# Rotating 96 images by 180 degrees: load packets of 64 KB and store packets of 32 KB, three on-chip columns and a scratch, instead of 32 KB and 16 KB with rotating tiles

## Chip, cores and metric

One core of one Trainium2 chip. The metric is the device time of one execution, in microseconds (us), as the median of several runs. Shorter is better. Terms: the DMA engines move data between HBM (the large memory) and the on-chip memory; in the traces they do so in packets, here of one row each; the span is the stretch of time that the profile covers.

## The reference

```python
def setup_inputs():
    batch, c, h, w = 32, 3, 256, 256
    return {"x": np.random.randn(batch, c, h, w).astype(np.float32)}

def reference(x):
    return np.rot90(x, k=2, axes=(-2, -1)).astype(np.float32)
```

Rotating an image by 180 degrees is the same as reversing the order of its 65,536 elements. There are 96 images of 256 KB: 25.17 MB are read from HBM and 25.17 MB written.

## The kernel before

Each of three passes takes 32 images. Every image is cut into 8 rows of 32 KB. Four of them are in tile `tinF`, the other four in reversed order in tile `tinB`, so that 32 x 4 rows fill the 128 partitions. VectorE copies half a row at a time with a negative step. Each half goes out as a store of its own (16 KB a row). Loads are issued on one queue (SyncE), stores on another (ScalarE).

```python
    NG = 32; Q = P // NG; S = 2 * Q; BLK = L // S; HB = BLK // 2
    x3 = x.rearrange("b c h w -> (b c) (h w)").rearrange("n (s e) -> n s e", s=S)
    o4 = out.rearrange("b c h w -> (b c) (h w)").rearrange(
        "n (s j f) -> n s j f", s=S, f=HB)
    tin_pool = ctx.enter_context(tc.tile_pool(name="tin", bufs=2))
    tout_pool = ctx.enter_context(tc.tile_pool(name="tout", bufs=4))
    for pp in range(n_pass):
        nsl = slice(pp * NG, (pp + 1) * NG)
        tinF = tin_pool.tile([P, BLK], x.dtype, tag="F")
        tinB = tin_pool.tile([P, BLK], x.dtype, tag="B")
        nc.sync.dma_start(out=tinF[:, :], in_=x3[nsl, 0:Q, :])
        nc.sync.dma_start(out=tinB[:, :], in_=x3[nsl, S - 1:Q - 1:-1, :])

        tF0 = tout_pool.tile([P, HB], x.dtype, tag="t")
        nc.vector.tensor_copy(out=tF0[:, :], in_=tinB[:, 2 * HB - 1:HB - 1:-1])
        nc.scalar.dma_start(out=o4[nsl, 0:Q, 0, :], in_=tF0[:, :])
        # [cut: the same for tB0 from tinF, tF1 from tinB, tB1 from tinF]
```

## Time and profile before

| | before |
|---|---|
| time, median (range), three runs | 123.76 us (123.72 to 123.96) |
| span in the profile | 122.3 us |
| VectorE busy | 27.2 us, 22% of the span |
| DMA queue 1 (loads) | 864 packets, 48.9% of the 16 DMA engines' span |
| DMA queue 10 (stores) | 1728 packets, 48.0% |
| HBM traffic | 50.33 MB, mean 412 GB/s |

The lines below are from the page of the kernel before: VectorE (DVE) busy time; the mean busy share of the DMA engines in 40 equal slices, in tenths; then for each DMA queue its packets, megabytes and share of the 16 engines' time.

```profile
DVE 27.2 (22%) x12; POOL 0.2 (0%) x4
...
DMA  5798989899999998999999999999999999999992
...
q1 hardware_dynamic: 864, 25.17, 48.9%
q10 hardware_dynamic: 1728, 25.17, 48.0%
```

The two shares add up to 97%: apart from the start and the end, the DMA engines are never free. Everything else must be read with that in mind. VectorE's waits are an example (the view of waits; total, number and longest, in us):

```profile
DVE tF L52 <- DMA tinB<-in_x_dram: 41.2, 2, 23.4
DVE tF L60 <- DMA out_dram<-tF: 14.7, 2, 12.2
DVE tB L56 <- DMA out_dram<-tB: 11.1, 2, 8.4
DVE tB L64 <- DMA out_dram<-tB: 7.6, 2, 5.0
DVE tF L52 <- DMA out_dram<-tF: 2.6, 1, 2.6
```

VectorE waits some 36 us for stores to free a tile. These waits look like something to remove, but while VectorE waits, the DMA engines are busy with what is already queued.

The trace keeps a start and a duration for every DMA packet. "Per engine" is a sum over all packets divided by 16.

### The profile page before, as it was taken

Reading aid. Unit: us, or ns where it says so; the run is one execution under the profiler, and the core shown is the slowest. Engines: PE = TensorE matmul, PEld = TensorE weight load, DVE = VectorE, ACT = ScalarE, POOL = GpSimd, SP = SyncE. Lnnn points to the kernel's source line nnn. Section 1 sums busy time; section 2 is a strip of 40 time slices with the busy share of each in tenths; the row PEclk is TensorE's granted clock in tenths of the full one; section 3 lists DMA queues with packets and bytes.
Section 4 is the critical chain, followed back from the end, with each engine's and each line's share of the span. In section 5 each row is a group of like instructions: output and inputs, shape, how many; then the busy total and the mean of one; then the engine's idle time right before and its main releaser. Section 6 shows DMA issues by size and latency. Waiting matters only on the chain.

```text
span 122.3 us, 93 instructions
## 1 busy us (share of the span) xinstructions
DVE 27.2 (22%) x12; POOL 0.2 (0%) x4
## 2 busy tenths in 40 slices
DVE  0000000399500000610160003307337156100000
POOL 0000000000000000000000000000000000000000
DMA  5798989899999998999999999999999999999992
GB/s 171 343 472 386 472 386 482 375 482 359 348 450 407 466 429 386 472 423 397 439 455 413 477 434 391 413 429 434 429 434 434 439 429 434 429 439 434 429 429 113
DMA packets 2592, 50.33 MB, mean 412 GB/s; under 512 B 288, under 2 KB 288, under 8 KB 288
## 3 DMA queue, kind: packets, MB, share of 16 engines
q1 hardware_dynamic: 864, 25.17, 48.9%
q10 hardware_dynamic: 1728, 25.17, 48.0%
HBM read 25.17 MB, written 25.17 MB: 412 GB/s over the span
## 4 chain that ended last, share of the span: by engine, by line
DMA 69%; DVE 11%; another core or an unknown queue 4%; SPq 0%; issue 0%; DVEq 0%
DMA out_dram<-tF 37%; DMA tinB<-in_x_dram 18%; DMA out_dram<-tB 14%; DVE tB L64 4%; DVE tF L60 4%; DVE tF L52 2%; DVE tB L56 2%; SPq L48 0%; DVEq L64 0%; DVEq L60 0%
## 5 line engine op out<-in xcount | busy, mean ns | idle before, releaser
L52 DVE COPY tF<-tinB 128x4096 f32<-128x4096 f32 x3 | 6.9, 2294 | 43.8 <-DMA tinB<-in_x_dram 41.2
L60 DVE COPY tF<-tinB 128x4096 f32<-128x4096 f32 x3 | 6.9, 2291 | 14.7 <-DMA out_dram<-tF 14.7
L56 DVE COPY tB<-tinF 128x4096 f32<-128x4096 f32 x3 | 6.9, 2292 | 11.1 <-DMA out_dram<-tB 11.1
L64 DVE COPY tB<-tinF 128x4096 f32<-128x4096 f32 x3 | 6.9, 2291 | 7.6 <-DMA out_dram<-tB 7.6
L80 POOL MEMSET const-bfloat16-1.0<- 128x1 bf16 x1 | 0.1, 102 | 0.0
L80 POOL MEMSET const-uint8-127<- 128x1 uint8 x1 | 0.1, 102 | 0.0
L80 POOL MEMSET const-float32-0.0<- 128x1 f32 x1 | 0.1, 99 | 0.2 <-issue 0.2
L80 POOL MEMSET const-float32-1.0<- 128x1 f32 x1 | 0.1, 99 | 0.0
## 6 DMA issues: line engine op xcount, KB each, us to landing
tinF<-in_x_dram SPq DMA_DIRECT2D x3, 4096.0 KB, 32.2
tinB<-in_x_dram SPq DMA_DIRECT2D x3, 4096.0 KB, 32.9
out_dram<-tF ACTq DMA_DIRECT2D x6, 2048.0 KB, 20.0
out_dram<-tB ACTq DMA_DIRECT2D x6, 2048.0 KB, 23.1
```

The costliest lines, as they stand in the source:

```text
L52: nc.vector.tensor_copy(out=tF0[:, :], in_=tinB[:, 2 * HB - 1:HB - 1:-1])
L56: nc.vector.tensor_copy(out=tB0[:, :], in_=tinF[:, 2 * HB - 1:HB - 1:-1])
L60: nc.vector.tensor_copy(out=tF1[:, :], in_=tinB[:, HB - 1::-1])
L64: nc.vector.tensor_copy(out=tB1[:, :], in_=tinF[:, HB - 1::-1])
L80: nc = _bacc.Bacc("TRN2", target_bir_lowering=False, num_devices=1)
```

## The change

The intent is larger packets and fewer waits. Each image is cut into 4 rows of 64 KB, so a group of 32 images fills a whole column of 128 x 64 KB. A row is loaded as one packet and stored as two of 32 KB. Three columns (A, B, C) and a scratch T hold everything: groups 0 and 2 are turned from A into C, group 1 inside B through T. The third load needs only the copies out of A, not a store.

```diff
-    x3 = x.rearrange("b c h w -> (b c) (h w)").rearrange(
-        "n (s e) -> n s e", s=S)
-    tin_pool = ctx.enter_context(tc.tile_pool(name="tin", bufs=2))
-    tout_pool = ctx.enter_context(tc.tile_pool(name="tout", bufs=4))
+    G = 32; E = L // 4; K = E // 4; J = E // 8      # [four lines joined]
+    x4 = x.rearrange("b c h w -> (b c) (h w)").rearrange(
+        "(g n) (s e) -> g (n s) e", n=G, s=4)
+    o4 = out.rearrange("b c h w -> (b c) (h w)").rearrange(
+        "(g n) (s e) -> g n s e", n=G, s=4)
+    # [cut: A, Bt, Ct are [P, E] tiles, T is [P, J], all from one pool with bufs=1]
+    # [cut: back(t, lo, hi) reads columns lo to hi backwards; copy is tensor_copy]
+    def load(t, g, lo=0, hi=E):
+        nc.sync.dma_start(out=t[:, lo:hi], in_=x4[g][:, lo:hi])
+    def store(t, g):
+        for lo in (0, E // 2):
+            nc.scalar.dma_start(out=o4[g][:, ::-1, lo:lo + E // 2],
+                                in_=t[:, lo:lo + E // 2])
+    def across(dst, src):
+        for c in range(0, E, K):
+            copy(dst[:, c:c + K], back(src, E - c - K, E - c))
+    def inside(t):
+        for lo in range(0, E // 2, J):
+            hi = E - lo - J
+            copy(T[:, :], back(t, hi, hi + J))
+            copy(t[:, hi:hi + J], back(t, lo, lo + J))
+            copy(t[:, lo:lo + J], T[:, :])
-    # [cut: the loop over passes]
+    load(A, 0)
+    load(Bt, 1)
+    across(Ct, A)
+    store(Ct, 0)
+    load(A, 2)
+    inside(Bt)
+    store(Bt, 1)
+    across(Ct, A)
+    store(Ct, 2)
```

## The prediction

> **What bounds it now.** The 16 DMA engines, nearly the whole span. The page's DMA queue part gives 48.9% of the 16 engines' 122.3 us span to the loads and 48.0% to the stores: 59.8 + 58.7 = 118.5 us per engine. VectorE is busy 27.2 us (22%). The trace's packet records show how regular this is: a 32 KB load packet takes 1.211 us, a 16 KB store packet 0.611 us, and 16 engines move 431 to 433 GB/s in every 4 us stretch from 8 to 120 us, except 28 to 36 us (388 and 382). The Trainium skill ("DMA: Bandwidth & Descriptors", Where 436 GB/s comes from) puts the ceiling at 435.2 GB/s; the trace agrees. So VectorE's waits for stores (14.7, 11.1, 7.6 and 2.6 us in the view of waits) and the loads' waits for stores are full queues, not idle engines: while one queue is held back the other uses the bandwidth. They cost nothing.
>
> Outside the packets: 2.1 us before the first one, 1.2 us from the last to the end, up to 1 us of unequal finish of the engines. Inside: the first packets are 0.58 us too long per engine, and load packets between 27 and 34 us, as the first stores join, lose 0.89 us per engine.
>
> **What the change does.**
> - Packets twice as large. From 0.611 and 1.211 us: 0.011 us per packet plus 0.600 us per 16 KB. 64 KB is then an estimated 2.411 us. Per engine: before 48 x 1.211 + 96 x 0.611 = 116.8 us; after 24 x 2.411 + 48 x 1.211 = 116.0 us. This saves 0.8 us, all on the critical path, since DMA is the critical path.
> - VectorE: 8 copies of 4096 columns (2.29 us each in the trace) and 12 of 2048 columns (estimate 1.22 us; the skill, "VectorE: DVE Perf Modes", perf-mode tier table, has 1227 ns for an fp32 copy of 2048). About 33 us instead of 27, none of it critical.
> - The third load waits only for the four copies out of A (issued near 32 us, instead of 46 us for the last load of before that had to wait for a store). Earlier issue buys nothing while the queues are full.
>
> **Does DMA run dry?** Mixed stretches of before show about 290 GB/s loads and 140 stores: packets alternate, so bytes go 2:1. The ratio stays. Then: A lands near 23 us, first stores issued 28 and 32, B lands near 50, B turned by about 65, third load lands near 80. At that moment some 9 MB of stores are still queued, 20 us of work, while half of C is ready again 5 us later. No gap, even if bytes were shared equally. The last stores are issued near 84 to 90 us, long before the drain at 120.
>
> **Prediction.** Span 121.3 us; time 122.7 us (before 123.76), range 121.8 to 123.7. Faster by over 2%: 0.05; within 2%: 0.92; slower: 0.03.
>
> **What would show it.** The page: 432 load and 864 store packets; load share of DMA time falling by about 0.3 us per engine, store share by about 0.5; rate 431 to 435 GB/s with no empty slice; third load issued near 32 us; VectorE near 33 us; the chain of waits nearly all DMA, ending in a store of C.
>
> **What would make it wrong.** 64 KB rows cut into two packets (saves only 0.5 us). The dip at 27 to 34 us growing with bigger packets, or vanishing (0.9 us more gain; I count a little of it). Stores starved behind 64 KB load packets, so that the backlog is spent before C's second turn: a gap of a few us. Reads and writes of larger blocks colliding in HBM, which the steady 433 GB/s gives no sign of.

## More of the kernel before

All runs told here are of the fast (undisturbed) state.

The next view cuts the span of the kernel before into stretches: from:to and length, VectorE and GpSimd busy time, granted clock, DMA share and GB/s.

```profile
6.00:26.00 20.00, 2.65 (x2) 0.00 (x0) 1.00 1.01 434
26.00:38.00 12.00, 6.25 (x3) 0.00 (x0) 1.00 0.98 390
36.00:46.00 10.00, 0.00 (x0) 0.00 (x0) 1.00 1.02 437
80.00:118.00 38.00, 11.47 (x5) 0.00 (x0) 1.00 1.01 432
```

Loads alone (6 to 26 us), the mix (36 to 46) and stores alone (80 to 118) all run near 434 GB/s. Only 26 to 38 us is slower, at full DMA share: the packets there take longer. This stretch is when the first stores begin, and it becomes important below. (A packet's bytes count where it starts, so these rates wobble by a few per cent, more with larger packets.)

The start, from the timeline (start, duration, engine, line, instruction). SPq is SyncE's queue, issuing:

```profile
0.73 0.60 SPq L48 DMA_DIRECT2D tinF<-in_x_dram  x1
1.38 0.59 SPq L49 DMA_DIRECT2D tinB<-in_x_dram  x1
```

The first load packet starts at 2.13 us.

## The result, and the profile after

| | before | after |
|---|---|---|
| time, median (range) | 123.78 us (123.72 to 123.96) | 123.31 us (123.28 to 123.51) |
| ratio of after to before | | 0.997, 95% interval 0.9955 to 0.9984 |
| span in the profile | 122.3 us | 121.7 us |
| VectorE busy | 27.2 us | 32.5 us |

A ratio here is the mean time of one kernel's fast runs over the mean time of the other's in the same rounds, so it isn't quite the ratio of the medians. The median of before has a fourth run here. The results are correct. The class forecast (within 2%) held and the time lies in the range, but of the 1.06 us forecast as the gain only 0.47 us came.

The same lines of the page of the changed kernel:

```profile
DVE 32.5 (27%) x20; POOL 0.2 (0%) x4
...
DMA  9779977998978999899998996999898989999992
...
q1 hardware_dynamic: 432, 25.17, 49.3%
q10 hardware_dynamic: 864, 25.17, 47.9%
```

There are half as many packets, as planned. But the loads' share of the engines' time, forecast to fall by 0.3 us per engine, rose: 48.9% of 122.3 us is 59.8 us, 49.3% of 121.7 us is 60.0 us. The stores fell from 58.7 to 58.3 us. The cause of the rise is the slow loads at the first stores, described below.

VectorE's waits in the changed kernel:

```profile
DVE Ct L53 <- DMA A<-in_x_dram: 36.8, 2, 22.8
DVE T L53 <- DMA Bt<-in_x_dram: 17.9, 1, 17.9
```

The 36 us of waits for stores are gone, and the time is only 0.47 us shorter. The same stretches of the changed kernel:

```profile
6.00:26.00 20.00, 3.21 (x2) 0.00 (x0) 1.00 0.97 419
26.00:38.00 12.00, 5.69 (x3) 0.00 (x0) 1.00 0.99 377
36.00:46.00 10.00, 0.00 (x0) 0.00 (x0) 1.00 1.02 442
80.00:118.00 38.00, 7.58 (x4) 0.00 (x0) 1.00 1.01 435
```

The stretch from 26 to 38 us is the slow one again, and lower: 377 instead of 390 GB/s. The start, from the timeline of the changed kernel:

```profile
0.73 0.37 SPq L56 DMA_DIRECT2D A<-in_x_dram  x1
1.15 0.42 SPq L56 DMA_DIRECT2D Bt<-in_x_dram  x1
```

The first load is issued in 0.37 us instead of 0.60 us, and its first packet starts at 1.73 us instead of 2.13 us.

Chaining each packet record to the one that starts where it ends gives the order on each of the 16 engines. Here is one engine of the changed kernel around the first stores (L load, S store, start + duration in us; worked out from the records):

```
L26.55+2.42 L28.96+2.42 L31.38+3.72 S35.10+1.21 L36.31+2.42 S38.73+1.21 L39.94+2.42
```

Loads and stores alternate row by row. The Trainium skill ("DMA: Bandwidth & Descriptors", Queues, rings and completion order) says that each engine goes round its queues packet by packet; the trace agrees, with one 64 KB row against one 32 KB row. The load just before the first store takes 3.72 us instead of 2.42 us, once, and nothing after it is slow. Ten of the 16 engines look like this. On the other six the loss is spread over the load before the first store and the load after it (3.02 to 3.21 us, then 3.11 to 3.49 us). I call it the first-store loss: the time by which packets between 6 and 45 us exceed the usual duration of their size, per engine.

A balance of the two traces, per engine, in us:

| | before | after | difference |
|---|---|---|---|
| first packet, mean of the engines | 2.48 | 2.05 | -0.43 |
| data packets, at their usual spacing | 116.34 | 116.01 | -0.33 |
| semaphore packets | 0.10 | 0.05 | -0.05 |
| slow first packets (before 6 us) | 0.58 | 0.57 | -0.01 |
| first-store loss | 0.89 | 1.44 | +0.55 |
| sum | 120.39 | 120.12 | -0.27 |
| end, mean of the engines, read | 120.40 | 120.12 | -0.28 |
| end of the last engine, read | 121.11 | 120.59 | -0.52 |

The sum meets the measured mean end within 0.01 us. The last engine gained 0.24 us more than the mean, as the engines happened to end closer together. "Usual spacing" is the time from one packet's start to the next on its engine: 0.607 us for 16 KB, 1.2095 for 32 KB and 2.415 for 64 KB. The usual durations in the records are 0.611, 1.213 and 2.418 us: each record overlaps the next by some 4 ns. This small thing turned out to be part of the prediction's first error. (The prediction's 1.211 us for 32 KB is not the usual one either: 684 of the 768 loads before have 1.213 us, and 7 have 1.211.)

### The profile page after: what moved, and what is told of

It reads as the page before. It is cut to its first block, busy times and chain, and to the rows that moved or that the text cites. A ratio compares the mean times of both kernels' runs of the same rounds, so it can differ in the third digit from the quotient of the medians.

```text
span 121.7 us, 78 instructions
## 1 busy us (share of the span) xinstructions
DVE 32.5 (27%) x20; POOL 0.2 (0%) x4
## 3 DMA queue, kind: packets, MB, share of 16 engines
q1 hardware_dynamic: 432, 25.17, 49.3%
## 4 chain that ended last, share of the span: by engine, by line
DMA 57%; DVE 13%; DVEq 2%; issue 0%
DMA A<-in_x_dram 57%; DVE Ct L53 13%; DVEq L108 2%; DVEq L53 0%
## 5 line engine op out<-in xcount | busy, mean ns | idle before, releaser
L53 DVE COPY Ct<-A 128x4096 f32<-128x4096 f32 x8 | 17.8, 2288 | 36.8 <-DMA A<-in_x_dram 36.8
L53 DVE COPY T<-Bt 128x2048 f32<-128x2048 f32 x4 | 4.9, 1228 | 18.0 <-DMA Bt<-in_x_dram 17.9
L53 DVE COPY Bt<-T 128x2048 f32<-128x2048 f32 x4 | 4.9, 1227 | 0.1
L53 DVE COPY Bt<-Bt 128x2048 f32<-128x2048 f32 x4 | 4.9, 1226 | 0.1
```

The costliest lines, as they stand in the source:

```text
L53: tc.keep_in_program_order(nc.vector.tensor_copy(out=dst, in_=src))
```

## The experiments

Theory: the packets gained little, the earlier start gained most, and the first-store loss took the packets' gain back. Rivals: the gain is the packets' or the schedule's; the loss comes with the new schedule, or with a fixed time. In the expectations, "packet sum" is the sum of durations (116.9 us before, 116.3 after), which still has the error just named in it; differences of 0.6 us there are 0.33 us in spacing. Sixteen runs were made, two of them repeats (e9 and e16), each beside the kernel before on its own chip (123.67 to 123.79 us).

### A tiny store first

```diff
+    Wt = pool.tile([P, 128], x.dtype, tag="W")
+    nc.vector.memset(Wt[:, :], 0.0)
+    nc.scalar.dma_start(out=o4[0][:, ::-1, 0:128], in_=Wt[:, :])
     load(A, 0)
```

> Changed kernel plus one 64 KB store of zeros (128 rows of 512 bytes, later overwritten) on the store queue at the start. In the changed kernel load packets lose 1.44 us per engine between 29 and 37 us, as the first store packets join (0.89 us in the kernel before); the rest of the packet sums came out as forecast. Theory A (the first use of the store queue, or the first write to HBM, costs each engine once): the loss moves to the start or goes; excess of load packets between 6 and 45 us below 0.3 us, time near 122.3 us. Theory B (full-size stores beginning beside a running load stream cost it): excess stays 1.2 to 1.6 us and time 123.3 to 123.5. Theory C (something at a fixed time, 27 to 35 us after the start): as B.

Measured: 123.58 us, ratio 1.000 (0.9986 to 1.0013). The loss was still 0.93 us, at the first large stores; the tiny packets themselves, between the loads from 7 to 22 us, cost nothing extra. Neither first use of the queue nor the first write by each engine is the whole cause: theory A falls. That 0.93 is lower than the 1.44 of the changed kernel agrees with no expectation.

### A tiny load on the store queue first

```diff
+    nc.scalar.dma_start(out=Wt[:, :], in_=x4[0][:, 0:128])
     load(A, 0)
```

> Changed kernel plus one 64 KB load (128 rows of 512 bytes) on the store queue at the start. If theory A holds because of the queue: the excess between 6 and 45 us goes here too, time near 122.3. If A holds because of the first write to HBM: it stays at 1.2 to 1.6 us here though the tiny store took it away. Theories B and C: stays, 123.3 to 123.5 us.

Measured: 123.53 us, ratio 0.999 (0.9977 to 1.0003), loss 1.22 us, as B and C expect. Both of these kernels also carry 128 extra packets of 0.027 us, 0.22 us per engine, which fits their being slower than the changed kernel.

### Small packets in the new schedule, twice

```diff
-        nc.sync.dma_start(out=t[:, lo:hi], in_=x4[g][:, lo:hi])
+        for a in (0, E // 2):
+            nc.sync.dma_start(out=t[:, a:a + E // 2], in_=x4[g][:, a:a + E // 2])
-        for lo in (0, E // 2):          # stores of E // 2 columns
+        for lo in range(0, E, E // 4):  # stores of E // 4 columns
         # [cut: the store's own lines, with E // 4 in place of E // 2]
```

> Changed kernel's columns and copies, but 32 KB load and 16 KB store packets as in the kernel before. Packet sum back to 116.9 us per engine (116.3 in the changed kernel). If the loss at the first stores grows with packet size: 0.7 to 1.0 us here and time within 0.2 us of the changed kernel (123.2 to 123.5). If it grew because of the new schedule: 1.4 us here, time 123.8 to 124.1.

> The changed kernel's schedule with packets of 32 and 16 KB once more, now as the measure for the two kernels above on the same chip. Packet sum 116.9 us, loss 0.8 to 1.0 us, time 0.2 to 0.5 us below the kernel before.

Measured: 123.25 us, ratio 0.9977 (0.9960 to 0.9994), loss 0.95 us; the second time 123.27 us, ratio 0.9964 (0.9952 to 0.9976), loss 1.02 us, just above its range. So the new schedule with the packets of before is as fast as the changed kernel (0.997, and 0.9960 below). Doubling the packets bought nothing that can be measured in the time here. Both runs start at 1.72 or 1.73 us, like the changed kernel.

### First stores 9 us later

```diff
     across(Ct, A)
+    across(Ct, A)
     store(Ct, 0)
```

> Changed kernel with the four copies into C made twice, so the first stores are issued about 9 us later (near 37 and 41 us instead of 27 and 32). Theories A and B: the slow load packets move from 29-34 us to about 38-44 us, excess 1.0 to 1.6 us, time unchanged within 0.3 us (123.0 to 123.6). Theory C (fixed time): they stay at 29 to 34 us.

Measured: 123.13 us, ratio 0.9960 (0.9948 to 0.9972). The loss is 1.18 us, all of it in the sixteen loads that start from 38.60 to 39.14 us, one on each engine. Its stretches:

```profile
26.00:38.00 12.00, 12.00 (x6) 0.00 (x0) 1.00 1.01 437
36.00:46.00 10.00, 5.85 (x4) 0.00 (x0) 1.00 1.09 419
```

From 26 to 38 us it runs at full rate, with VectorE busy all the time. The loss moved with the stores: a fixed time (C) falls, and so does any disturbance by VectorE's copies. That the time did not rise shows again that an earlier store or third load buys nothing while DMA has work.

### One queue

```diff
-            nc.scalar.dma_start(out=o4[g][:, ::-1, lo:lo + E // 2],
+            nc.sync.dma_start(out=o4[g][:, ::-1, lo:lo + E // 2],
```

> Changed kernel with the stores issued on the loads' queue, in program order: loads of A and B, stores of C, load of A, stores of B, stores of C. No store packet is ever between load packets. The delayed runs showed that the slow load packets move with the first stores, and an early tiny store or load doesn't take them away. Theory B (stores beginning beside a running load stream cost about 1.2 us once): no slow load packet after 6 us, time 1.0 to 1.4 us below the changed kernel, 121.9 to 122.4 us. Rival D (any first change from reading HBM to writing it costs that): a slow packet or a gap of about 1 us near 42 us, where the first store follows the loads, time 123.0 to 123.5.

Measured: 123.28 us (122.86 to 124.31), ratio 0.9975 (0.9942 to 1.0008). The profiled run is the slowest of these, as its last engine ends 1.35 us after the mean of the engines. There is a loss of 1.27 us in the last loads before the first stores at 42 us, although no store was ever between loads. Its stretches:

```profile
26.00:38.00 12.00, 5.76 (x3) 0.00 (x0) 1.00 1.01 437
36.00:46.00 10.00, 2.27 (x2) 0.00 (x0) 1.00 1.01 383
58.00:76.00 18.00, 0.80 (x1) 0.00 (x0) 1.00 1.00 435
```

Theory B, sharing between two queues, falls. D holds in one half: the first change from reading to writing costs this. The second such change, near 81 us after 20 us of loads alone, lost only 0.11 us. So it is not every change.

### Other store packets: 64 KB, and 16 KB with 64 KB loads

```diff
-        for lo in (0, E // 2):           # two stores of E // 2 columns
+        # 64 KB: one store of E columns; 16 KB: four stores of E // 4 columns [lines cut]
```

> Changed kernel with one 64 KB store packet for a row instead of two of 32 KB. Theory B1 (what is lost is about one store packet's time for each engine, as the engine takes in store data ahead of its turn): excess 1.8 to 2.6 us, and with 0.2 us saved by fewer packets the time rises to 123.6 to 124.5. Theory B2 (a loss that doesn't depend on the store packet): excess 0.9 to 1.4 us, time 122.9 to 123.3.

> Changed kernel with 64 KB load packets but 16 KB store packets. Packet sum 0.4 us above the changed kernel (48 x 0.611 x 2 against 48 x 1.213). Theory B1: excess 0.7 to 1.0 us as in the kernels with 32 KB loads and 16 KB stores, time as the changed kernel. If the load packet sets it: 1.2 to 1.4 us, time 0.4 us above the changed kernel.

Measured: with 64 KB 123.34 us, ratio 0.9985 (0.9952 to 1.0018), loss 1.20 us; with 16 KB 123.28 us, ratio 0.9963 (0.9948 to 0.9977), loss 0.90 us. Sixteen KB fits B1, 64 KB doesn't: the loss grows from 16 to 32 KB and, in the one run with 64 KB, no more.

### 32 KB loads with 32 KB stores

```diff
-        nc.sync.dma_start(out=t[:, lo:hi], in_=x4[g][:, lo:hi])
+        for a in (0, E // 2):
+            nc.sync.dma_start(out=t[:, a:a + E // 2], in_=x4[g][:, a:a + E // 2])
```

> Changed kernel with 32 KB load packets and its own 32 KB store packets. Packet sum 116.4 us. If the store packet sets the loss at the first stores: 1.1 to 1.4 us, time within 0.3 us of the kernel with 32 and 16 KB of this call, either way. If it is the sum of both packets or the load packet: 0.8 to 1.0 us, time 0.4 us below that kernel.

Measured: 123.71 us, ratio 0.9996 (0.9980 to 1.0011), loss 1.29 us. Against small packets with the same loads on the same chip (loss 1.02 us, 123.27 us) the larger store packets raise the loss by 0.27 us, as the first expectation has it. The time is 0.44 us higher, more than the 0.3 us that I had allowed. The two traces' engines end at the same time in the mean (120.01 and 119.95 us), and the last one 0.26 us later. The rest of the difference stays open.

### The kernel before with shuffled rows

```diff
-        nc.sync.dma_start(out=tinF[:, :], in_=x3[nsl, 0:Q, :])
+        nc.sync.dma_start(out=tinF[:, :], in_=x2[r0:r0 + P, :])   # 128 rows in a row
-        nc.scalar.dma_start(out=o4[nsl, 0:Q, 0, :], in_=tF0[:, :])
+        nc.scalar.dma_start(out=o4[nB, ::-1, 0, :], in_=tF0[:, :]) # 16 images x 8 rows
 # [cut: the second load and the other three stores likewise]
```

> The kernel before, its packets, tiles, pools and order kept, but each load takes 128 consecutive 32 KB rows, so its pattern has two dimensions instead of three (results are right: the halves of an image now share a tile). In the kernel before the first load's issue takes 0.60 us and its first packet starts at 2.13 us; in the changed kernel 0.37 and 1.73 us, and so in all runs with the two-dimensional load. Theory: the start alone is the changed kernel's gain: first packet at 1.7 to 1.8 us, packet sum and slow packets as in the kernel before (116.9 and 0.9 us), time 0.3 to 0.5 us below before, as low as the changed kernel. Rival (gain of the packets or schedule): start 2.1 us, or no gain in time.

Measured: 131.51 us, ratio 1.060 (1.055 to 1.064). It failed as a test. The start did move to 1.71 us, but the altered stores spoiled the rest. From the GB/s line of its page (40 slices):

```profile
GB/s 162 487 365 446 487 365 446 487 324 461 335 466 411 451 385 431 441 461 390 426 431 431 441 406 370 309 319 324 360 375 411 406 436 431 416 446 426 365 203 41
```

Once only stores are left, the rate falls to 309 GB/s for a while, and at the end the engines run out at different times (mean 124.47, last 128.10 us). These stores have 16 images by 8 rows where the others have 32 by 4. The next run has the same loads with the old stores and is not slow, so the stores are what costs this; why, I did not pursue.

### The kernel before with only its loads altered

Everything else is kept; the result is wrong, as the rows land elsewhere.

```diff
-        "n (s e) -> n s e", s=S)
+        "n (s e) -> (n s) e", s=S)
-        nc.sync.dma_start(out=tinF[:, :], in_=x3[nsl, 0:Q, :])
-        nc.sync.dma_start(out=tinB[:, :], in_=x3[nsl, S - 1:Q - 1:-1, :])
+        nc.sync.dma_start(out=tinF[:, :], in_=x3[2 * pp * P:(2 * pp + 1) * P, :])
+        nc.sync.dma_start(out=tinB[:, :], in_=x3[(2 * pp + 1) * P:(2 * pp + 2) * P, :])
```

> The kernel before with only its loads altered: each takes 128 consecutive rows of 32 KB, a pattern of two dimensions instead of three; everything else is the same, so the result is wrong on purpose. Theory (the changed kernel's gain is its earlier start): load issue 0.4 us instead of 0.6, first packet at 1.7 us instead of 2.1, packet sum and slow packets as in the kernel before (116.9 and 0.9 us), time 0.3 to 0.5 us below before, level with the changed kernel of this call within 0.2 us. Rival (the packets gave the gain): time as before, within 0.15 us.

Measured: 123.19 us, ratio 0.9955 (0.9938 to 0.9972), level with the changed kernel (123.21 us). Loss 0.80 us. Its start:

```profile
0.73 0.37 SPq L48 DMA_DIRECT2D tinF<-in_x_dram  x1
1.15 0.42 SPq L49 DMA_DIRECT2D tinB<-in_x_dram  x1
```

VectorE's waits for stores are those of the kernel before:

```profile
DVE tF L60 <- DMA out_dram<-tF: 14.7, 2, 12.2
DVE tB L56 <- DMA out_dram<-tB: 11.1, 2, 8.5
DVE tB L64 <- DMA out_dram<-tB: 7.6, 2, 5.1
```

This run shows that the start is enough. With the packets, tiles, pools, waits and order of before, altered loads alone give as much as the change gave. It also reads the rows in another order, but that is not where the time went: its engines end 0.43 us earlier in the mean than those of before (119.97 against 120.40 us) and its first packets come 0.45 us earlier (2.03 against 2.48), while slow first packets (+0.08) and first-store loss (-0.09) cancel. In the two small-packet runs the rows don't follow each other in memory, and they start as early, which points to the two dimensions and not the order. The converse, the changed kernel with the late start, was not run.

### The changed kernel again, and larger stores of zeros first

```diff
+    nc.vector.memset(T[:, :], 0.0)                    # 8 KB a row; the other run: 512 columns, 2 KB
+    nc.scalar.dma_start(out=o4[0][:, ::-1, 0:J], in_=T[:, :])
     load(A, 0)
```

> The changed kernel unaltered, as a second sample on this chip beside the three others. Excess of load packets at the first stores 1.2 to 1.4 us (1.44 in its first profile), packet sum 116.26, start 1.73 us, time 0.35 to 0.5 us below the kernel before.

> Changed kernel plus a store of zeros of 128 rows of 8 KB (1 MB, later overwritten) on the store queue at the start. What is known so far: slow load packets of 0.9 to 1.4 us per engine come just before the first large store packets, move with them, come in one queue too (there the run of stores that followed 20 us of loads alone had only 0.11), and stay at 0.93 after 64 KB in rows of 512 bytes. Theory D1 (once in an execution, with the first writes to HBM of some size): 0.5 to 1.2 us beyond the usual 0.6 in the first 10 us, and under 0.3 us at 29 to 37 us. Time: changed kernel plus 2.4 us for the extra 1 MB, less up to 0.6. Theory D2 (each time large stores begin after loads alone): some loss in the first 10 us and again 0.9 to 1.4 at 29 to 37 us; time plus 2.4 us or more.

> The same with rows of 2 KB (256 KB, 0.6 us of DMA). D1: between the two, 0.3 to 0.9 us left at 29 to 37 us, time 0.2 to 0.6 us above the changed kernel. D2: 0.9 to 1.4 us left, time 0.6 us or more above it.

Measured: the changed kernel again 123.21 us, ratio 0.9960 (0.9943 to 0.9976), loss 1.25 us. With 8 KB rows 125.37 us: 0.68 us in the first packets, no more than other runs have (0.54 to 0.75), then 0.27 us between 18 and 30 us and 0.69 us at the first large stores. With 2 KB rows 123.66 us, loss 0.90 us, all at the large stores. Neither D1 nor D2 holds as written: an early megabyte shrinks the later loss, but to half, and a part of it appears elsewhere.

### An on-chip copy before the first store

```diff
     across(Ct, A)
+    nc.scalar.dma_start(out=T[:, :], in_=Ct[:, 0:J])
     store(Ct, 0)
```

> Changed kernel with a copy of 1 MB from one on-chip tile to another (128 rows of 8 KB) on the store queue just before the first store. It takes some 8 turns between load packets, so the first packets to HBM come near 50 us instead of 32. If the loss belongs to a second stream, or to reading from the chip's memory: slow load packets (0.5 us or more in all) before the first copy packets, at 27 to 34 us, little near 50. If it belongs to writing HBM: under 0.2 us at 27 to 34 us and 0.8 to 1.4 us near 45 to 53 us. Time: changed kernel plus 2.4 us either way.

Measured: 125.29 us, ratio 1.0133. Loss 0.16 us from 28 to 38 us, 0.31 us from 38 to 46 us while only copy packets alternate with loads, and 0.38 us from 46 to 56 us, at the first packets to HBM; 0.85 us in all. Neither expectation fits: more than half of the loss (0.47 us) came before the first data packet to HBM, so writing HBM isn't the only cause, but a share came with the HBM stores.

### A version with small packets first

```diff
-        for lo in (0, E // 2):
+        cuts = (0, E // 4, E // 2, E) if g == 0 else (0, E // 2, E) if g == 2 else (0, E)
+        for lo, hi in zip(cuts, cuts[1:]):
```

> Changed kernel whose first half group is stored in 16 KB packets, the middle group in 64 KB packets, the rest as it was. Packet sum 116.2 to 116.3 us. If the first store packets' size sets the loss: 0.8 to 1.0 us at 27 to 37 us, time 122.7 to 123.0 us, 0.6 to 0.9 % below the kernel before. If not: 1.2 us and 123.1 to 123.3 us.

Measured: 123.05 us (122.70 to 123.48), ratio 0.9953 (0.9937 to 0.9968), loss 0.83 us. The loss came out as forecast, the time 0.05 us above its range. Its median is the lowest of all, below both kernels; against the changed kernel (0.997 and 0.9960, on other chips) the intervals overlap, so that part is not shown.

The losses by store packet, for the runs whose stores begin with large ones beside the loads:

| first stores | first-store loss, us per engine |
|---|---|
| 16 KB packets (before; e3, e16, e7, e12, e14) | 0.89; 0.95, 1.02, 0.90, 0.80, 0.83: mean 0.90 |
| 32 KB packets (changed kernel twice; e2, e4, e13) | 1.44, 1.25; 1.22, 1.18, 1.29: mean 1.28 |
| 64 KB packets (e6) | 1.20 |

Here e stands for the experiments in the order of their numbers: e2 tiny load, e3 and e16 small packets, e4 late store, e6 and e7 other store packets, e12 before with altered loads, e13 32 KB loads, e14 small packets first. Each is one profiled run. The one queue (e5, 32 KB) had 1.27 us and the shuffled rows (e8, 16 KB) 0.80. The runs with a smaller store or a copy first don't follow the table: 0.93 (e1) and 0.90 us (e11) with 32 KB packets, the level of 16 KB; 0.96 (e10, in two parts) and 0.85 (e15).

## Why the prediction was right or wrong

- **Right: what bounds the kernel, and no gap.** "They cost nothing", it said of the waits for stores. The kernel before with altered loads kept them (14.7, 11.1 and 7.6 us) and was as fast as the changed kernel without them, and delaying the first store by 9 us cost no time. The third load was issued at 31.7 us (forecast near 32), B landed by 49.6 us (near 50), the third load by 78.6 us (near 80), VectorE's busy time was 32.5 us (about 33), and its copies of 2048 columns took 1.23 us each: the 1227 ns that the Trainium skill gives ("VectorE: DVE Perf Modes", perf-mode tier table) is met.
- **Wrong: "0.011 us per packet", so "This saves 0.8 us".** This is the term that was mis-sized. It was the difference of recorded durations. With the usual 1.213 us in place of 1.211 it is 0.009 us, and of that 0.004 us is the overlap of the records. From the spacing of starts, 2 x 0.607 - 1.2095 gives 0.0045 us per packet, and 72 packets fewer per engine save about 0.33 us. The skill could have warned of it ("DMA: Bandwidth & Descriptors", Why small descriptors are slow): it gives about 3 cycles of overhead per packet inside the DMA engine; if they are cycles of the 850 MHz in its section Where 436 GB/s comes from, which the page doesn't say, that is an estimated 3.5 ns. The trace has 4.5 ns.
- **Wrong: "The dip at 27 to 34 us growing ... or vanishing (0.9 us more gain; I count a little of it)".** It was named as a risk, and the sign of what I counted was wrong. The dip grew by 0.55 us in this pair of profiles, by 0.38 us in the means of the table (0.90 to 1.28 us). That is as much as the packets saved. The table shows that it goes with the size of the first store packets (16 KB against 32 KB), not with the schedule or the load packet; with a smaller store put first it was back at the level of 16 KB (0.93 and 0.90 us), and why is open.
- **Missed: the start.** "2.1 us before the first one" was carried over unchanged. The first packet came 0.40 us earlier, as a load pattern of two dimensions is issued in 0.37 us instead of 0.60 (0.23 us of the 0.40; the rest is a shorter wait from the end of the issue to the first packet, 0.63 instead of 0.80 us). The altered loads in the old kernel show that this alone gives as much as the whole change.
- **What follows for the sum.** Forecast: 0.8 us from packets and about 0.2 us from the dip. Measured: packets 0.33 us, given back by the first-store loss, and 0.4 us from the start that had not been forecast. That the time still lies in the range owes something to luck: without the start that was not forecast it would have been an estimated 123.7 us (123.31 + 0.40), the upper edge of the range.
- **Open: what the first-store loss is.** Excluded by runs as the whole cause: a fixed time, VectorE's copies, the first use of a queue, an engine's very first small write, sharing between two queues, and every change from loads to stores alike. What is left is a cost that is paid about once as the first large packets leave the on-chip memory, smaller with smaller packets and after an earlier store (0.93 us after 64 KB, 0.69 us after a megabyte), and paid in part by an on-chip copy. An engine that fills itself once with store data ahead of their turn would look like that, but that is only argued: 64 KB packets don't raise it, and it appears in a single queue too.

## What to carry to other kernels

Where the DMA engines are busy 97% of the span, as here, ask first whether waits for buffers are only the queue being full; removing them gained nothing here. Look at the edges instead, the first issue and the first packet. Take a per-packet cost from the spacing of starts, not from durations, and multiply it by the number of packets saved before believing in larger packets: beyond 16 and 32 KB only 0.3% was left. When a gain is small, check whether it comes from the part of the change that was meant; here it came from one dimension less in the load pattern.

## What the Trainium skill lacked or had wrong

- "DMA: Bandwidth & Descriptors" doesn't say that issuing a load of three dimensions takes longer than one of two: 0.60 against 0.37 us for the first 128 rows of 32 KB (before, and before with altered loads), and the first packet 0.4 us earlier. Its figure of about 600 ns to the first byte (Latency and other measured facts) fits the changed kernel (0.63 us from the end of the issue to the first packet) but not the kernel before (0.80 us), if it is counted from the end of the issue, which the page doesn't say.
- No page has the first-store loss: 0.80 to 1.02 us per engine with 16 KB store packets, 1.18 to 1.44 us with 32 KB, once as large stores begin, 0.90 and 0.93 us with 32 KB after a smaller store, 0.11 us at a later change from loads to stores.
- No page says that DMA packet records overlap by about 4 ns, so that the cost of a packet from the usual durations (0.009 us) is twice that from spacing (0.0045 us). The page's about 3 cycles (an estimated 3.5 ns at 850 MHz) is near the latter.
- "DMA: Bandwidth & Descriptors" has 435.2 GB/s as the fabric's ceiling; 16 engines at one 64 KB packet every 2.415 us move 434 GB/s, reading or writing, so the trace agrees. The HBM limit of about 358 GB/s that the same section says binds transfers between HBM and the on-chip memory did not bind this one core.
- The same page doesn't say that stores of 16 images by 8 rows run slower than 32 by 4: 309 GB/s at worst against 432 (the kernel before, 80 to 118 us).
